# Weight sums of a seven-product matrix multiplication: which engine makes them, and the order in which they are asked for and used

## The chip, the cores and the metric

The kernel runs on one core of a Trainium2 chip. The metric is the device time of one execution in microseconds (us); it is the median over three runs. One further execution was recorded by the hardware profiler, and all rows of the profile come from that one.

## The reference

One layer of a streaming encoder for 512 frames of width 2048, in fp32. Cut to what matters:

```
h = rms_norm(x);  proj = h @ w_in
y_a = banded softmax attention (16 heads of 64, own chunk of 64 frames + 8 before)
y_g = rms_norm(gated linear attention (4 heads)) * silu(r_g)
x = x + concat(y_a, y_g) @ w_out
u = causal_depthwise_conv(rms_norm(x) @ w_ffn_up);  x = x + (gelu(u_gate) * u_val) @ w_ffn_down
x = x + sigmoid(rms_norm(x) @ w_ple_gate) * (p @ w_ple_proj)
out = rms_norm(x)
```

The matrix products are the bulk. The change concerns how the weights of some of them are prepared.

## The kernel before, in words

**A unit.** A large product is cut into units. Each unit multiplies a 2 x 2 block of weights (L11, L12, L21, L22, each 128 x 1024 values, in the down stages dn1 and dn2 128 x 896) by the stage's activations, and does so with seven products in place of eight (PRODUCTS, ahead of line 32). The products use four weight sums and seven operands that are formed once per stage:

```
P1: L11 R11   P2: L12 R21   P6: S2 N2   P5: S1 N1   P7: S3 T3   P3: S4 R22   P4: L22 T4
S1 = L21 + L22    S2 = S1 + L11    S3 = L21 + L11    S4 = S2 + L12
```

The order of the products is PLAIN (line 32): P1, P2, P6, P5, P7, P3, P4. Every weight or sum is split into a high part (`wh`, made by ScalarE, called ACT in the profile) and a low part (`wl`, the difference, made by VectorE, called DVE). A product is three passes of 8 matmuls (7 in dn1 and dn2) on TensorE (PE) into one of the accumulators accA, accB and accC.

**How a sum is made.** A unit has one of three modes, `sums`:
- "dma": SyncE (SP) loads L21 into a page, and GpSimd (POOL) issues a DMA that accumulates L22 (for S1) or L11 (for S3) onto it; so L21 comes in twice. S2 and S4 are added by VectorE.
- "dve": each L is loaded once, and VectorE adds all four sums (`make`, from line 415).
- "s3": as "dve", but S3 is made by a DMA of POOL that accumulates L11's page onto L21's page.

**Pages and the order of the loads.** Raw weights and sums live in pages of a small ring. NEEDS (line 356) gives, for each mode, the order in which a unit asks for its pages; the lists of all units are put one after another in `wanted`. `issue` (line 389) takes the next entry when a page is free and issues its load on SP and, for S1 and S3 in mode "dma", the accumulation on POOL right behind it (lines 404 to 407). A name with a star is a page that is reserved for VectorE's result. `used` (line 409) gives a page back when the last of its uses has been issued. So the order of the loads hangs on NEEDS, and the time at which each may start hangs on when VectorE or ACT has finished with an older page.

**The order of the work.** The list `steps` holds the (unit, product) pairs in order. The engines' programs are written by hand in that order: two steps ahead of a product its weights are split (`prep_high`, from line 446, then `prep_low`), one step ahead of that the next sum is added (`make`), and after a product its accumulator is collected by ACT or VectorE. An `agenda` places everything else at a step: the softmax, the stores, the loads and splits of the next stage's operands. The first two and the last two units of most stages are done in pairs, with the products of both alternating.

**The stages.** `pp` (a small projection, two units), then the front "in" with 12 units (0 to 7 give the attention's values, keys and queries, and each is followed by the softmax of its heads; 8 to 11 give the gates), `pp` again, then `wo` (output projection), `up` (44 units), `dn0`, `dn1`, `dn2` (down projection in three chunks of 8 units), and `pg` (the last gate). Before them stands the gated linear attention, in plain matmuls. The next stage's operands are loaded in the buffers that the present stage's operands leave; a load of operand T3 for `wo` waits until P7 of the front's last unit has read the old T3. A split of such an operand occupies ACT and VectorE at the step that the agenda gives it (lines 856 to 868 for the stages from `wo` on).

**Modes before.** All 12 front units are "dma". In the stages dn0 to dn2 the first two and the last two units are "dma" and the rest are "dve" (lines 832 to 834).

Of the kernel before, what the change touches and what calls it, by code (L numbers as in the profile page):

```python
# [29 lines left out]
            "P7": ("S3", "T3", "A"), "P3": ("S4", "R22", "C"), "P4": ("L22", "T4", "A"),  # L30
            "PP": ("L11", None, None)}
PLAIN = ("P1", "P2", "P6", "P5", "P7", "P3", "P4")
HALVES = ("P1", "P2", "P6", "P7", "P4", "P5", "P3")
RINGS = {"wr": ("r0", "r1", "r2"), "wh": ("h0", "h1", "h2"), "wl": ("l0", "l1", "l2")}
FRONT_RINGS = {"u": ("u0", "u1"), "c": ("c0",), "x": ("r6",)}
# [6 lines left out]
def encoder_block(ctx: ExitStack, tc: tile.TileContext, A, out):  # L42
# [13 lines left out]
    class InOrder:  # L56
        def __init__(self, engine):
            self.engine, self.on = engine, False
# [44 lines left out]
    late = []  # L103
# [103 lines left out]
    def xslot(i, name):  # L207
        return pairs[i % 8][:, i // 8, :]
# [7 lines left out]
    first = xslot(0, "x0_0")  # L216
# [50 lines left out]
    def scratch(name, shape):  # L267
        return dp.tile(list(shape), F32, name=name)
# [44 lines left out]

    class Stage:
        def __init__(self, name, units, kb, xd, weights, after, sums, edge, last=PLAIN, begin=None, begin_at=0,
                     chained=False, pace=None, late=(), single=False):
            self.name, self.kb, self.xd, self.weights, self.after = name, kb, xd, weights, after
            self.begin, self.begin_at, self.pace, self.late = begin, begin_at, pace, late
            self.chained, self.tail, self.quarter = chained, [None, None], None
            self.n = (4, kb - 4 - 2 * chained)  # L320
            self.x = {}
            n = len(units)
            self.units = [Unit(self, u, last if i >= n - 2 else PLAIN, edge if i < 2 or i >= n - 2 else sums)
                          for i, u in enumerate(units)]
            for i in range(n):
                self.units[i].pos = i
            if single:
                self.groups = [[u] for u in self.units]
                return
            self.units[0].first = True  # L330
            for i in range(2):
                self.units[i].head = i
                self.units[n - 2 + i].last = i
            self.groups = [self.units[:2]] + [[u] for u in self.units[2:-2]] + [self.units[-2:]]
# [7 lines left out]
        def split(self, op, g, body=True, tails=(0, 1)):  # L342
# [6 lines left out]
            if self.chained and g == 1:  # L349
# [4 lines left out]


    NEEDS = {"dma": ("L11", "L12", "S1", "S2*", "S3", "L22"), "dve": ("L11", "L12", "L21", "L22", "S1*", "S2*"),
             "s3": ("L11", "L12", "L21", "L22", "S1*", "S2*")}

    class Unit:
        def __init__(self, stage, u, order, sums):  # L360
            self.stage, self.u, self.order, self.sums = stage, u, order, sums
            self.first, self.head, self.last = False, None, None
            self.w, self.tag = {}, {}
            if sums == "dma":
                self.uses = dict(L11=2, L12=2, S1=2, S2=2, S3=1, L22=1)
                self.made = {"S2", "S4"}
            else:
                self.uses = dict(L11=3, L12=2, S1=2, S2=2, L21=2, L22=2)
                self.made = {"S1", "S2", "S3", "S4"}
            self.parts = dict(C11=2, C12=2, C22=2, C21=1)  # L370
            self.have = set()
            self.left = dict(A=4, B=1, C=2)
            self.o = None
            self.banks = {}
# [40 lines left out]
    def make(unit, name):  # L415
        if name not in unit.made:
            return
        unit.made.discard(name)
        n = unit.stage.kb * P
        w = lambda q: unit.w[q][:, :n]  # L420
        if name == "S1":
            vec.tensor_tensor(made_page(unit, "S1")[:, :n], w("L21"), w("L22"), ALU.add)
            used(unit, "L21")
            used(unit, "L22")
            if unit.sums == "s3":
                unit.made.discard("S3")
                nc.gpsimd.dma_start(w("L21"), w("L11"), accum_op=ALU.add)
                used(unit, "L11")
        elif name == "S2":
            make(unit, "S1")  # L430
            vec.tensor_tensor(made_page(unit, "S2")[:, :n], w("S1"), w("L11"), ALU.add)
            used(unit, "S1")
            used(unit, "L11")
        elif name == "S3":
            make(unit, "S1")
            if "S3" in unit.made or unit.sums == "dve":
                vec.tensor_tensor(w("L21"), w("L21"), w("L11"), ALU.add)
                used(unit, "L11")
        else:
            vec.tensor_tensor(w("S2"), w("S2"), w("L12"), ALU.add)  # L440
            used(unit, "L12")
# [4 lines left out]
    def prep_high(i, own=None):  # L446
        if i >= len(steps):
            return None
        unit, prod = steps[i]
        name = PRODUCTS[prod][0]  # L450
        n = unit.stage.kb * P
        make(unit, name)
        if prod == unit.order[0] and unit.sums != "dma":
            make(unit, "S1")
        if i + 1 < len(steps):
            nxt, p = steps[i + 1]
            q = PRODUCTS[p][0]
            if (nxt is unit or nxt.paired) and (q != "S4" or "P6" in nxt.w):
                make(nxt, q)
        if i > 0 and steps[i - 1][1] == "P6" and steps[i - 1][0].paired:  # L460
            make(steps[i - 1][0], "S4")
        key = {"S4": "S2"}.get(name, "L21" if name == "S3" and unit.sums != "dma" else name)
        raw = unit.w[key]
        hi, lo = own or (page("wh", "wh", F32R), page("wl", "wl", F32R))
        act.activation(hi[:, :n], raw[:, :n], AF.Copy)
        unit.w[prod] = hi, lo
        return unit, key, hi[:, :n], lo[:, :n], raw[:, :n]
# [66 lines left out]
    def load_x(src, unit):  # L534
        unit.xs = page("c", "xs").rearrange("p (s t) -> p s t", s=2)
        nc.sync.dma_start(unit.xs, src[unit.u])
# [106 lines left out]
    def after_gate(unit):  # L643
# [9 lines left out]
                    begin=lambda u: load_x(streams[0], u), begin_at=6, chained=True)]  # L653
# [13 lines left out]
    h1d = operand_scratch("h1", 8)  # L667
# [152 lines left out]
    def front_weights(u, q):  # L820
        j = {"1": u, "2": 8 + u}[q[1]] if u < 8 else 24 + 2 * (u - 8) + (q[1] == "2")
        return A["w_blk"][j, int(q[2]) - 1]

    front = Stage("in", list(range(12)), 8, h1d, front_weights, lambda u: (attend if u.u < 8 else after_gates)(u), "dma",
                  "dma", single=True)
    embed = [Stage("pp", us, 8, None, lambda u, q: A["w_ple_proj"][u], lambda u: [], "dma", "dma", single=True)
             for us in ([0, 1], [2, 3])]
    for u in embed[0].units + embed[1].units:
# [1 line left out]
    mids = streams[1:3] + [scratch("x2d_", (8, P, 2, T)), streams[3]]  # L830
    for ci, n in enumerate(CHUNKS):
        stages.append(Stage(f"dn{ci}", list(range(8)), n // 2, gd[ci], blk2(A[f"w_dn{ci}"]),
                            after_add(mids[ci + 1]) if ci < 2 else after_norm(streams[3], h3d, nple),
                            "dve", "dma", begin=lambda u, s=mids[ci]: load_x(s, u), begin_at=0 if ci else 8, late={}))
    stages.append(Stage("pg", list(range(8)), 8, h3d, blk2(A["w_ple_gate"]), after_gate, "dma", "dma", last=HALVES,
                        begin=load_gate, begin_at=9, chained=True, pace=(15, 5.3), late={}))
    stages[4].quarter = last_quarter(lambda: stages[8], nple)
# [7 lines left out]
    for st in stages:  # L845
        for group in st.groups:
            base[group[0]] = base[group[-1]] = len(steps)
            steps += [(u, p) for p in group[0].order for u in group]
            for u in group:
                u.paired = len(group) > 1  # L850
            need = [[(u, name) for name in (NEEDS[u.sums] if u.stage not in embed else ("L11",))] for u in group]
            wanted += [e for es in zip(*need) for e in es]
# [3 lines left out]
    for a, b in zip(stages[3:], stages[4:]):  # L856
        i0 = base[a.units[-1]]
        for n, p in enumerate(PLAIN):
            op = PRODUCTS[p][1]
            for g in range(2):  # L860
                start = 2 * n + 2 + g
                if g and b.chained:
                    start = max(start, 5)
                at = 2 * n + (11 if g else 8)
                if g and b.chained and op in ("R21", "T4"):
                    at = max(at, 15)
                agenda[i0 + start].append((0, lambda b=b, op=op, g=g: b.load(op, g)))
                agenda[i0 + at].append((3, lambda b=b, op=op, g=g: b.split(op, g)))

    i0 = base[front.units[-1]]  # L870
    for n, op in enumerate(("T3", "R22", "T4")):
        for g in range(2):
            agenda[n + g * (n == 2)].append((3, lambda op=op, g=g: front.split(op, g)))
    for n, p in enumerate(PLAIN):
        op = PRODUCTS[p][1]
# [4 lines left out]
        at, k = ((8, 1), (8, 1), (9, 1), (12, 1), (11, 3), (12, 3), (13, 3))[n]  # L880
# [80 lines left out]
    end = len(steps) - 14  # L961
# [6 lines left out]
    for n in range(2):  # L968
        u = stages[-1].units[n - 2]
# [292 lines left out]
    for i, (unit, prod) in enumerate(steps[:-4]):  # L1262
# [19 lines left out]
        if i - len(steps) in EARLY:  # L1282
            p, op, g = EARLY[i - len(steps)]
# [8 lines left out]
        elif prod == unit.order[-1]:  # L1292
            begin = i + 1
            if st.pace:
                begin = max(begin, base[st.units[0]] + int(st.pace[0] + st.pace[1] * unit.pos))
# [167 lines left out]
```

## Time and profile before

| | us |
|---|---|
| median of three runs | 2304.75 (2300.37 to 2307.55) |
| the profiled execution | 2304.32 |
| its span, first to last instruction | 2302.6 |
| TensorE busy | 2261.4 (98%) |
| VectorE busy | 1888.0 (82%) |
| ScalarE busy | 1300.7 (56%) |
| mean granted TensorE clock | 0.993 |

A group row of the profile reads: line, engine, operation, what is written from what with its shape, count, then total busy us and mean ns of one, then the idle time of the engine just before these instructions and what ended most of it. Line 64 is the line of the helper that records the instructions in order, so that nearly all compute instructions carry it; they are told apart by the tiles that they write and read (`s` is a page with S1 or S3 made by DMA or S2 or S4 made by VectorE; `l` a page with a loaded L; `u` a unit's result; `sc` the softmax's scores; `ptr` transposes of them on TensorE). In the rows of waits stand who waited, for what, the total, how often, and the longest. In the chain of waits stand the start in us, the duration, and what the chain passed through. In the rows of the busy times in a stretch, the numbers behind the stretch's bounds are its length, then each engine's busy time with the count of instructions, then the granted clock, the busy share of the DMA engines and GB/s.

### The profile page before, as it was taken

To read this page: it belongs to the slowest core of one execution; us is meant where nothing else is said; L and a number is where in the kernel's file an instruction comes from. 1 tells how busy PE (TensorE), PEld (TensorE's weight loads), DVE (VectorE), ACT (ScalarE), POOL (GpSimd) and SP (SyncE) were. 2 spreads that over 40 slices of the span, in tenths; PEclk is the share of its full clock that TensorE was granted. 3 is DMA by queue.
4 is the path that set the end of the run, shared out by engine and by line. 5 is a ranking of instruction groups with operands and counts; after the bars stand their busy time and mean duration, and the time that the engine had idled before them with its cause. 6 is when DMAs were issued, how large, how long until landed. Compare 5 with 4: busy or idle time off the path is not lost.

```text
span 2302.6 us, 44996 instructions
## 1 busy us (share of the span) xinstructions
PE 2261.4 (98%) x18016; PEld 2189.7 (95%) x18016; DVE 1888.0 (82%) x2590; ACT 1300.7 (56%) x1908; POOL 144.0 (6%) x181
## 2 busy tenths in 40 slices
PE   9999999999999999999999999999999999999996
PEld 8888889999989999999999999999999999999996
DVE  7566458998788888998888888888898787998986
ACT  6354456776565665555555555555564554656655
POOL 0000000000000100000000000000000100000000
PEclk9999999999999999999999999999999999999999
DMA  6623586667978977787878787777866967879994
GB/s 217 204 74 110 183 271 166 186 182 200 309 251 257 327 214 211 207 221 205 227 197 219 204 222 211 215 208 217 272 207 231 309 216 255 268 254 329 268 292 163
DMA packets 195569, 516.77 MB, mean 224 GB/s; under 512 B 20928, under 2 KB 72384, under 8 KB 195360
## 3 DMA queue, kind: packets, MB, share of 16 engines
q1 hardware_dynamic: 166080, 422.37, 52.5%
q0 software_dynamic: 23616, 84.95, 21.2%
q10 hardware_dynamic: 5664, 6.59, 0.8%
q8 instruction: 141, 2.31, 0.4%
q14 instruction: 68, 0.56, 0.1%
HBM read 435.18 MB, written 76.55 MB: 222 GB/s over the span
## 4 chain that ended last, share of the span: by engine, by line
PE 87%; DVE 6%; DMA 3%; ACT 3%; issue 2%; DVEq 0%; ACTq 0%; POOLq 0%; SPq 0%
PE accA L64 40%; PE accC L64 21%; PE accB L64 10%; PE v L252 3%; PE v L254 3%; PE v L253 3%; DVE wl L64 1%; DMA s<-in_w_blk 1%; PE py L64 1%; PE ptr L64 1%; PE psc L64 1%; DVE s L64 1%; DMA s<-in_w_out 1%; DVE u L64 1%; DVE xs L64 1%
## 5 line engine op out<-in xcount | busy, mean ns | idle before, releaser
L64 DVE TENSOR_TENSOR wl<-s,wh 128x1024 fp32r<-128x1024 f32 (+1 forms) x365 | 437.9, 1200 | 65.8 <-ACT wh L64 65.0
L64 ACT ACTIVATE wh<-l 128x1024 fp32r<-128x1024 f32 (+1 forms) x308 | 319.1, 1037 | 184.7 <-PE accC L64 118.0
L64 DVE TENSOR_TENSOR wl<-l,wh 128x1024 fp32r<-128x1024 f32 (+1 forms) x308 | 367.8, 1194 | 61.0 <-ACT wh L64 60.6
L64 ACT ACTIVATE wh<-s 128x1024 fp32r<-128x1024 f32 (+1 forms) x365 | 377.7, 1036 | 34.2 <-DVE s L64 15.8
L64 ACT ACTIVATE u<-accA 128x256 f32<-128x256 f32 x290 | 109.6, 378 | 365.4 <-PE accA L64 365.4
L64 DVE TENSOR_TENSOR s<-s,l 128x1024 f32<-128x1024 f32 (+1 forms) x192 | 229.7, 1196 | 8.5 <-DMA s<-in_w_blk 8.5
L64 PE MATMUL accA<-up_T,wh 128*128 128x256 f32 x1408 | 178.8, 279 | 0.0
L64 PEld LDWEIGHTS accA<-up_T,wh 128*128 128x128 f32 x1408 | 170.3, 188 | 0.0
L64 DVE SCALAR_TENSOR_TENSOR cv<-u,cw,cv 128x511 f32<-128x511 f32 (+1 forms) x176 | 131.7, 749 | 3.1
L407 POOL DMA_DIRECT2D s<-in_w_up x88 | 75.3, 856 | 787.9 <-DMA s<-in_w_up 383.6
L252 PE MATMUL v<-wv_h,h 128*128 128x512 f32 x256 | 100.2, 391 | 0.1
L254 PE MATMUL v<-wv_h,h 128*128 128x512 f32 x256 | 100.2, 391 | 0.0
L253 PE MATMUL v<-wv_l,h 128*128 128x512 f32 x256 | 99.7, 389 | 0.0
L64 PE MATMUL accA<-up_T,wl 128*128 128x256 f32 x704 | 96.6, 279 | 0.0
L64 PE MATMUL accA<-dn_T,wh 128*128 128x256 f32 x704 | 91.5, 282 | 4.1 <-ACT wh L64 4.1
L64 PE MATMUL accB<-up_R,wh 128*128 128x256 f32 x704 | 91.6, 282 | 2.0 <-DVE up_R L64 1.3
L64 PEld LDWEIGHTS accA<-dn_T,wh 128*128 128x128 f32 x704 | 86.8, 191 | 4.7 <-ACT wh L64 4.7
L64 PE MATMUL accA<-up_R,wh 128*128 128x256 f32 x704 | 89.8, 280 | 0.0
L64 PE MATMUL accC<-up_R,wh 128*128 128x256 f32 x704 | 89.4, 279 | 0.0
L64 PE MATMUL accA<-up_N,wh 128*128 128x256 f32 x704 | 89.4, 279 | 0.0
L64 PE MATMUL accC<-up_N,wh 128*128 128x256 f32 x704 | 89.4, 279 | 0.0
L64 PEld LDWEIGHTS accB<-up_R,wh 128*128 128x128 f32 x704 | 86.7, 190 | 2.7 <-DVE up_R L64 1.6
(401 smaller groups left out, 5070.6 us busy)
## 6 DMA issues: line engine op xcount, KB each, us to landing
l<-in_w_up SPq DMA_DIRECT2D x132, 512.0 KB, 5.5
s<-in_w_up SPq DMA_DIRECT2D x88, 512.0 KB, 4.9
s<-in_w_up POOLq DMA_DIRECT2D x88, 512.0 KB, 6.2
l<-in_w_dn SPq DMA_DIRECT2D x56, 448.0 KB, 5.7
l<-in_w_blk SPq DMA_DIRECT2D x36, 512.0 KB, 4.7
l<-in_w_out SPq DMA_DIRECT2D x28, 512.0 KB, 5.1
l<-in_w_dn SPq DMA_DIRECT2D x28, 512.0 KB, 5.3
s<-in_w_blk SPq DMA_DIRECT2D x24, 512.0 KB, 4.6
```

The source lines that it names most:

```text
L64: ins = f(*args, **kw)
L252: nc.tensor.matmul(ps[t], h1[kt][:, 0, sl], wh, start=kt == 0, stop=False)
L253: nc.tensor.matmul(ps[t], h1[kt][:, 0, sl], wl, start=False, stop=False)
L254: nc.tensor.matmul(ps[t], h1[kt][:, 1, sl], wh, start=False, stop=kt == KD - 1)
L407: nc.gpsimd.dma_start(t, src("L22" if name == "S1" else "L11"), accum_op=ALU.add)
```

## The change

It has three parts.
1. Front units 0 to 7 get the mode "first": all as in "dma", but the page for S1 is asked for ahead of L11 and L12.
2. Front units 8, 9 and 10 become "dve", unit 11 becomes "s3". Seven accumulating DMAs and four loads of 512 KB go, and VectorE makes seven more additions.
3. In all front units, and in the first two units of dn0, dn1 and dn2, P3 and P7 change places (order LATE_S3: P1, P2, P6, P5, P3, P7, P4). In the down stages the splits of R22 and T3 change places with them; the loads of these operands keep their order.

The number of matmuls, and of instructions on ScalarE, stays as it is.

```diff
 PLAIN = ("P1", "P2", "P6", "P5", "P7", "P3", "P4")
+LATE_S3 = ("P1", "P2", "P6", "P5", "P3", "P7", "P4")
...
         def __init__(self, name, units, kb, xd, weights, after, sums, edge, last=PLAIN, begin=None, begin_at=0,
-                     chained=False, pace=None, late=(), single=False):
+                     chained=False, pace=None, late=(), single=False, head=PLAIN, end=()):
...
-            self.units = [Unit(self, u, last if i >= n - 2 else PLAIN, edge if i < 2 or i >= n - 2 else sums)
+            how = [edge] * 2 + [sums] * (n - 4) + [edge] * 2
+            how[n - len(end):] = end
+            self.head = head
+            self.units = [Unit(self, u, head if i < 2 or single else last if i >= n - 2 else PLAIN, how[i])
                           for i, u in enumerate(units)]
...
     NEEDS = {"dma": ("L11", "L12", "S1", "S2*", "S3", "L22"), "dve": ("L11", "L12", "L21", "L22", "S1*", "S2*"),
+             "first": ("S1", "L11", "L12", "S2*", "S3", "L22"),
              "s3": ("L11", "L12", "L21", "L22", "S1*", "S2*")}
...
-            if sums == "dma":
+            if sums in ("dma", "first"):
                 self.uses = dict(L11=2, L12=2, S1=2, S2=2, S3=1, L22=1)
...
-        if prod == unit.order[0] and unit.sums != "dma":
+        if prod == unit.order[0] and unit.sums in ("dve", "s3"):
             make(unit, "S1")
...
-        key = {"S4": "S2"}.get(name, "L21" if name == "S3" and unit.sums != "dma" else name)
+        key = {"S4": "S2"}.get(name, "L21" if name == "S3" and unit.sums in ("dve", "s3") else name)
...
-    front = Stage("in", list(range(12)), 8, h1d, front_weights, lambda u: (attend if u.u < 8 else after_gates)(u), "dma",
-                  "dma", single=True)
+    front = Stage("in", list(range(12)), 8, h1d, front_weights, lambda u: (attend if u.u < 8 else after_gates)(u), "first",
+                  "first", single=True, head=LATE_S3, end=("dve", "dve", "dve", "s3"))
...
-                            "dve", "dma", begin=lambda u, s=mids[ci]: load_x(s, u), begin_at=0 if ci else 8, late={}))
+                            "dve", "dma", begin=lambda u, s=mids[ci]: load_x(s, u), begin_at=0 if ci else 8, late={}, head=LATE_S3))
...
-                at = 2 * n + (11 if g else 8)
+                at = 2 * b.head.index(p) + (11 if g else 8)
```

## The prediction

> **What bounds the kernel now.** I read the page first, then the waits of TensorE and VectorE, then the chain of waits around the longest of them, and last the busy time in short stretches.
>
> ```profile
> span 2302.6 us, 44996 instructions
> ...
> PE 2261.4 (98%) x18016; PEld 2189.7 (95%) x18016; DVE 1888.0 (82%) x2590; ACT 1300.7 (56%) x1908; POOL 144.0 (6%) x181
> ...
> PE 87%; DVE 6%; DMA 3%; ACT 3%; issue 2%; DVEq 0%; ACTq 0%; POOLq 0%; SPq 0%
> ```
>
> TensorE bounds the kernel: it is idle for 2302.6 - 2261.4 = 41.2 us, and nothing in the change alters a matmul. So the change can only take away or add idle time of TensorE, or time at a lower clock. The profiled run took 2304.3 us, 1.7 us beyond its span and 0.4 us below the median of 2304.75 us; I carry each change in microseconds over to the median. 0.3% (6.9 us, about what a measurement of this kernel can tell from no change) is a sixth of all idle time there is.
>
> ```profile
> PE accA L64 <- ACT wh L64: 4.1, 3, 3.0
> ...
> PE ptr L64 <- DVE sc L64: 2.0, 1, 2.0
> PE ptr L64 <- DVE mx L64: 2.0, 3, 1.6
> ...
> DVE s L64 <- DMA s<-in_w_blk: 8.5, 3, 4.1
> ```
>
> Two of these belong to sums that an accumulating DMA makes: the longest wait on ACT's wh (3.0 us), and VectorE's waits on in_w_blk (8.5 us), which reach TensorE as the 2.0 us on sc. The chain of waits shows both; first the front, in its second and third unit:
>
> ```profile
> 335.52 6.73 DMA s<-in_w_blk
> 342.34 1.24 DVE s L64
> ...
> 354.69 7.25 DMA s<-in_w_blk
> ...
> 366.11 0.50 DVE sc L64
> 366.65 1.25 PE ptr L64 x8
> ```
>
> VectorE's add S2=S1+L11 stands behind the landing of S1 at 342.3 and again at 361.9. What is queued behind it on VectorE, the softmax's sc included, comes late, and the transposes ptr start late. The second place is the head of dn2, product P7 of its second unit:
>
> ```profile
> 1984.44 7.84 DMA s<-in_w_dn
> 1992.35 0.96 ACT wh L64
> 1993.36 3.99 PE accA L64 x21
> ```
>
> S3 lands at 1992.3, ACT splits it 1 us later, and TensorE starts at 1993.36. The busy times in the stretches around both (core's columns: length, PE, PEld, DVE, ACT, POOL, granted clock, DMA share, GB/s):
>
> ```profile
> 364.60:368.00 3.40, 1.39 (x11) 1.12 (x11) 3.26 (x12) 2.43 (x7) 0.00 (x0) 1.00 0.36 139
> 368.00:371.41 3.41, 3.41 (x18) 3.41 (x18) 3.27 (x13) 3.41 (x9) 0.00 (x0) 0.50 0.02 5
> 371.41:374.80 3.39, 3.39 (x37) 3.09 (x37) 3.29 (x12) 2.73 (x10) 0.00 (x0) 1.00 0.55 142
> ...
> 1989.40:1992.80 3.40, 0.99 (x9) 0.79 (x7) 0.01 (x1) 0.45 (x1) 0.00 (x0) 1.00 0.98 316
> 1992.80:1996.20 3.40, 2.84 (x13) 2.85 (x14) 2.87 (x3) 3.40 (x6) 0.00 (x0) 0.50 0.33 84
> ```
>
> Each stall is followed by 3.4 us at half clock: 18 matmuls where the next 3.39 us hold 37. So a stall costs itself and up to half of 3.41 us: at the front 2.0 + 1.7 = 3.7 us, in dn2 3.0 + 2.84 / 2 = 4.4 us.
>
> **Part 1: S1 asked for first (front units 0 to 7).** SP's load of L21 for S1 moves past the loads of L11 and L12, and POOL's accumulation behind it starts that much sooner. The order in which a unit's pages are asked for puts S1 three product steps ahead of before, 8.4 us or more by this row for one product (the next rows are the landings):
>
> ```profile
> 319.65 2.80 PE accA L64 x24
> ...
> s<-in_w_blk SPq DMA_DIRECT2D x24, 512.0 KB, 4.6
> ...
> l<-in_w_blk SPq DMA_DIRECT2D x36, 512.0 KB, 4.7
> ```
>
> VectorE's longest wait was 4.1 us, so all go, and TensorE's 2.0 us with the half clock: -3.7 us. Bounds: -2.0 if the clock drops all the same, -3.7. What comes late next is L11, now behind 512 KB more; a unit's seven products alone take 7 x 2.80 = 19.6 us, against 4.7 us to landing, so I leave it at nothing. If it did land late, ACT's split of it and then P1, the first product, would be held once in each unit, with all that ACT and VectorE have queued behind.
>
> **Part 2: P3 ahead of P7 in the front.** S4 = S2+L12 is wanted one product sooner, and its add (1.2 us by the row below) moves on VectorE ahead of the softmax's normalisation; ACT's split of S4 moves with it, S3's back. No instruction is added. The stretch rows tell how much room VectorE has:
>
> ```profile
> 370.00:550.00 180.00, 180.00 (x1619) 174.72 (x1618) 162.00 (x404) 130.79 (x268) 11.96 (x14) 1.00 0.69 184
> ...
> 550.00:644.00 94.00, 90.87 (x718) 86.53 (x717) 69.92 (x119) 58.53 (x92) 6.19 (x8) 0.98 0.90 282
> ...
> L64 DVE TENSOR_TENSOR s<-s,l x192: 1082/1218/1226, 319.6 to 2249.5; 128x1024 f32<-128x1024 f32 x160, 128x896 f32<-128x896 f32 x32
> ...
> L64 DVE TENSOR_TENSOR s<-l,l x16: 1083/1152/1221, 678.1 to 2054.8; 128x1024 f32<-128x1024 f32 x8, 128x896 f32<-128x896 f32 x8
> ```
>
> In steady attention TensorE never idles while VectorE is 90% busy (162 of 180 us). What stands behind the moved add comes 1.2 us later unless VectorE had a gap; the bounds are 0 and 7 units x 1.2 = 8.4 us. The 18 us of gaps are twice the work moved, so I take a value near 0: a twelfth, +0.7.
>
> **Part 3: gate units 8 to 11 sum on VectorE.** Seven accumulations leave POOL and four loads leave SP, 11 transfers of 512 KB; VectorE gains seven adds of 1.15 to 1.22 us, 8.3 us in all (unit 11's S3 stays a DMA of POOL, now from one page to another). From 550 to 644 it has 24 us free, but not evenly:
>
> ```profile
> 540.13 1.22 DVE L64 TENSOR_TENSOR wl<-s,wh 128x1024 fp32r<-128x1024 f32 x1
> ...
> 541.24 0.81 PE L64 MATMUL ptr<-ident,sc 128*128 128x128 f32 x6
> ...
> 562.12 1.23 DVE L64 TENSOR_TENSOR u<-u,on 128x1024 f32<-128x1024 f32 x1 [2.01 <-ACT u L64]
> ...
> 569.40:572.80 3.40, 1.59 (x11) 1.15 (x11) 3.26 (x10) 2.83 (x7) 0.00 (x0) 1.00 1.03 364
> 572.80:576.20 3.40, 3.40 (x18) 3.40 (x17) 1.61 (x2) 0.25 (x1) 0.85 (x1) 0.50 1.04 333
> ```
>
> Units 8 and 9 are prepared while the last softmaxes still run: ptr at 541 follows VectorE's normalisation within 1 us, and around 571 TensorE already waits for VectorE (1.8 us idle, then half clock). Four of the adds (S1 and S3 of both units) fall there, 4.8 us; the one gap of 2.0 us takes some. Bounds: 0 (all in gaps) and 4.8 plus one more half-clock stretch, 6.5. I take 2.2, nearer the low end because 24 us are free in the whole stretch; the three adds of units 10 and 11 fall after the softmaxes and cost nothing. L22 is now needed for the first sum, and VectorE waits with it if it lands late; that is inside the bounds.
>
> [...]
>
> **Part 4: the start of wo.** wo's load of T3 waits until the front's last unit has used that buffer in P7, now one product (2.8 us) later, and SP's loads of R22 for wo queue behind it. Against it stand the 11 transfers less before.
>
> ```profile
> 644.00:660.00 16.00, 12.13 (x95) 11.13 (x94) 16.00 (x24) 12.32 (x22) 0.64 (x1) 1.00 0.81 253
> ...
> PE accA L64 <- DVE wl L64: 2.4, 2, 1.3
> ```
>
> TensorE is idle for 3.9 us here with VectorE busy in all 16.0 us, so VectorE is the limit and the transfers come second. Bounds: -3.9 and +2.8; I take 0.
>
> **Part 5: P3 ahead of P7 in the first two units of each down stage.** In dn2 P7 of the second unit moves back by one pair of products, 2 x 21 matmuls, or 2 x 21/24 x 2.80 = 4.9 us. P7 would come at about 1993.4 - 3.0 + 4.9 = 1995.3; S3 landed 3.0 us before that, and ACT's split of it took 0.96 us. The stall and its half clock go: -4.4 us (0 if S4 or R22 is late instead). R22's split takes T3's slot on ACT and T3's goes later; SP's loads keep their order. In dn1's head TensorE never idles, though VectorE is busy for 23.6 of 24 us (first row): 0. The other rows are for dn0:
>
> ```profile
> 1836.00:1860.00 24.00, 24.00 (x208) 24.00 (x207) 23.61 (x28) 16.82 (x23) 0.00 (x0) 1.00 0.94 302
> ...
> 1692.00:1701.00 9.00, 6.92 (x53) 6.11 (x52) 8.36 (x10) 7.41 (x10) 0.00 (x0) 1.00 0.38 137
> ...
> 1676.72 1.04 ACT L64 ACTIVATE dn_T<-dn_T 128x1024 fp32r<-128x1024 f32 x1
> ...
> L340 SPq DMA_DIRECT2D dn_R<-g_R x2: 319/428/538, 1663.8 to 1664.3; - x2
> ...
> dn_R<-g_R SPq DMA_DIRECT2D x2, 512.0 KB, 13.2
> ```
>
> R22's split moves into the slot at 1676.72 that T3 had, while R22 lands about 13.2 us after 1663.8, at 1677: no margin, and ACT would hold the next unit's wh for a few tenths. TensorE's 2.1 us of idle time lie under VectorE's 93%, and the exchange takes no work from VectorE. Bounds -2.1 and +1.5; I take 0.
>
> **Sum.** -3.7 + 0.7 + 2.2 + 0 - 4.4 + 0 = -5.2 us: 2299.1 us against the profiled run, 2299.5 against the median. Its own range is -8.1 + 2.9 with parts 2 to 4 varied by 3 either way: 2296.5 to 2302.5.
>
> **Rivals.** (a) VectorE has room everywhere: parts 2 and 3 cost nothing, and the emptier queues give back half of wo's 3.9 us. Then -8.1 - 1.9 = -10.0 us, 2294.7 (2292.7 with all of it). For it: 24 us free from 550 to 644; against: the 571 stall. (b) Slower: VectorE takes the bound from TensorE in the front. If S4's add shows in full in seven attention units (7 x 1.2 = 8.4) and the four adds of units 8 and 9 too (4.8), that is 13.2 - 8.1 = +5.1 us, 2309.9, with one half-clock stretch more 2311.6. It decides once 8.1 of these 13.2 us show on TensorE; the 10% VectorE has free speak against it, the late softmax at 366 and 571 for it. (c) In the down stages the wait only changes its name: P3 waits for R22 or S4 as P7 did for S3. Then part 5 gives nothing: -0.8 us, 2304.0. R22's margin in dn0 speaks for it; dn2, where VectorE was idle (0.01 of 3.40 us), against. (d) The clock drops do not come from the stalls, so only 2.0 + 3.0 go: -5.0 + 2.9 = -2.1, 2302.7. Against it stand both pairs of rows. [...]
>
> **How the numbers follow.** Forecast 0.40, (a) 0.34, (b) 0.14, (c) 0.08, (d) 0.04. Below 2297.8 (-0.3%) lie (a) and 0.08 of the forecast's own range: faster 0.42. Above 2311.7 lie the worse part of (b), with L11 or R22 late on top, and little else: slower 0.12. The rest, 0.46, is within 0.3%. The range runs from (a) with all of wo's idle time, just above 2292.5, to 2308.0 between the forecast and (b).
>
> **What would show it.** Right: VectorE's wait on in_w_blk under 1 us, no clock drop at 368 or at dn2's head, TensorE waiting 1 to 3 us more for sc, mx or PT between 540 and 575, seven adds of 1.15 to 1.22 us more. Wrong: waits on l<-in_w_blk before a unit's P1; TensorE idle in steady attention by more than 2 us; waits for dn_R or s in the heads of dn0 to dn2; wo's start idle by under 2 or over 6 us.

## The result: slightly slower, outside the range

The changed kernel is slower: the ratio to the kernel before is 1.0024, with a 95% interval of 1.0012 to 1.0035, that is +5.5 us (2.8 to 8.1). The medians over 22 runs each are 2313.35 us (2305.42 to 2318.23) and 2310.86 us (2299.14 to 2315.35). The forecast was 2299.5 us with a range of 2292.5 to 2308.0.

The median of before stood at 2304.75 us over its first three runs; repeated runs of one kernel spread over some 16 us, and 7 us of that can come from a stage that the change leaves alone (last section). So besides the ratios I compare profiles stage by stage, a stage being taken from the start of its first matmul to that of the next stage's. For example, from two views by tile (engine, operation, count: duration in ns, first and last start in us), first before, then after:

```profile
L64 PE MATMUL accA<-in_R,wh x192: 277/279/282, 319.5 to 608.1; 128*128 128x256 f32 x192
...
L64 PE MATMUL accA<-wo_R,wh x128: 277/280/282, 638.6 to 766.1; 128*128 128x256 f32 x128
```

```profile
L65 PE MATMUL accA<-in_R,wh x192: 277/280/283, 319.2 to 614.1; 128*128 128x256 f32 x192
...
L65 PE MATMUL accA<-wo_R,wh x128: 277/280/281, 646.5 to 773.0; 128*128 128x256 f32 x128
```

The front (with the small projection behind it) took 638.6 - 319.5 = 319.1 us before and 646.5 - 319.2 = 327.3 us after. From the page, one row of before, then after:

```profile
L64 DVE TENSOR_TENSOR s<-s,l 128x1024 f32<-128x1024 f32 (+1 forms) x192 | 229.7, 1196 | 8.5 <-DMA s<-in_w_blk 8.5
```

```profile
span 2313.8 us, 44976 instructions
...
PE 2269.6 (98%) x18016; PEld 2197.8 (95%) x18016; DVE 1899.3 (82%) x2597; ACT 1301.5 (56%) x1908; POOL 138.0 (6%) x174
...
L65 DVE TENSOR_TENSOR s<-s,l 128x1024 f32<-128x1024 f32 (+1 forms) x192 | 229.6, 1196 | 0.9 <-DMA s<-in_w_dn 0.7
```

The change does what it says: seven more instructions on VectorE, seven fewer on POOL, and VectorE's idle time in front of its adds on the accumulating DMA fell from 8.5 to 0.9 us. TensorE's waits tell where the loss is (the first row is before, the others after):

```profile
PE accC L64 <- ACT u L64: 0.5, 1, 0.5
```

```profile
PE accC L65 <- ACT u L65: 6.3, 6, 3.8
...
PE accA L65 <- DVE u L65: 4.0, 4, 1.9
...
PE ptr L65 <- DVE mx L65: 3.1, 3, 1.6
```

The waits on sc and on ACT's wh (2.0 and 4.1 us before) are gone, as forecast, and the softmax waits 3.1 us for VectorE's mx (2.0 before). In the place of the former stand two groups that before were 0.5 us (on accC) and absent (on accA): accC behind ACT's u, and accA behind VectorE's u. `u` is the unit's result, so these are matmuls that wait until the product before them has been taken out of the accumulator. The table of products says why. Each accumulator is summed up over several products: P3 is added onto P5's result in accC, and P4 onto P7's in accA, and in between the partial sum has to be read out. In PLAIN the last products take accC, accA, accC, accA by turns; in LATE_S3 they are accC, accC, accA, accA. The engine that reads out then works while TensorE stands still.

How long depends on what that engine has queued. TensorE, VectorE at P4 of a gate unit (timelines, of the same execution):

```profile
583.57 1.09 PE L65 MATMUL accA<-in_T,wl 128*128 128x256 f32 x8
586.53 3.42 PE L65 MATMUL accA<-in_T,wh 128*128 128x256 f32 x16 [1.87 <-DVE u L65]
```

```profile
582.24 1.22 DVE L65 TENSOR_TENSOR s<-l,l 128x1024 f32<-128x1024 f32 x1
583.37 0.75 DVE L65 TENSOR_TENSOR tp<-yp 128x256 f32<-128x256 f32 x2
584.04 0.88 DVE L65 SCALAR_TENSOR_TENSOR tp<-tp,yp 128x256 f32<-128x256 f32 x2
584.84 1.22 DVE L65 TENSOR_TENSOR wl<-l,wh 128x1024 fp32r<-128x1024 f32 x1
585.97 0.41 DVE L65 TENSOR_TENSOR u<-u,accA 128x256 f32<-128x256 f32 x1
```

P7 ends at 584.66. VectorE is on a run of older work, one of the new additions (s<-l,l) in it, and reaches the 0.41 us read of accA at 585.97. The longest such wait is at the head of dn0, where ACT takes P5 out of accC:

```profile
1708.52 0.63 ACT L65 ACTIVATE cv<-cv 128x512 f32<-128x512 f32 x1 [1.58 <-DVE cv L65]
1709.05 1.04 ACT L65 ACTIVATE dn_T<-dn_T 128x1024 fp32r<-128x1024 f32 x1
1710.00 0.36 ACT L65 ACTIVATE u<-accC 128x256 f32<-128x256 f32 x1
```

```profile
1705.53 1.10 PE L65 MATMUL accC<-dn_N,wl 128*128 128x256 f32 x8
1710.41 3.45 PE L65 MATMUL accC<-dn_R,wh 128*128 128x256 f32 x16 [3.78 <-ACT u L65]
```

Even with two units in alternation, ACT reaches the read only after the last conv work of the stage up and an operand's split. And two of these stalls cost clock besides (columns as in the prediction); the wait of 2.4 us at the last gate unit's P4, at 632, cost none (granted clock 1.00 from 628 to 634.8):

```profile
583.60:587.04 3.44, 1.57 (x14) 1.39 (x13) 3.41 (x7) 1.06 (x1) 0.00 (x0) 0.98 0.99 320
587.04:590.45 3.41, 3.41 (x18) 3.41 (x18) 1.61 (x2) 0.00 (x0) 0.00 (x0) 0.52 0.75 238
1706.50:1709.91 3.41, 0.13 (x2) 0.00 (x0) 3.02 (x4) 1.83 (x3) 0.00 (x0) 1.00 0.25 97
1709.91:1713.32 3.41, 2.90 (x13) 2.91 (x14) 3.16 (x4) 3.41 (x6) 0.00 (x0) 0.50 0.41 154
```

### The profile page after: what moved, and what is told of

Read it like the earlier page. It is cut to its first block, busy times and chain, and to the rows that moved or that the text cites. A ratio compares the mean times of both kernels' runs of the same rounds, so it can differ in the third digit from the quotient of the medians.

```text
span 2313.8 us, 44976 instructions
## 1 busy us (share of the span) xinstructions
PE 2269.6 (98%) x18016; PEld 2197.8 (95%) x18016; DVE 1899.3 (82%) x2597; ACT 1301.5 (56%) x1908; POOL 138.0 (6%) x174
## 4 chain that ended last, share of the span: by engine, by line
PE 85%; DVE 6%; ACT 4%; DMA 3%; issue 1%; ACTq 0%; SPq 0%; DVEq 0%
PE accA L65 40%; PE accC L65 21%; PE accB L65 10%; PE v L253 3%; PE v L255 2%; PE v L254 2%; DVE wl L65 2%; PE py L65 1%; ACT wh L65 1%; DVE s L65 1%; DVE u L65 1%; PE psc L65 1%; PE ptr L65 1%; DMA xs<-x1d 1%; DMA x3d<-xs 0%
## 5 line engine op out<-in xcount | busy, mean ns | idle before, releaser
L65 DVE TENSOR_TENSOR wl<-s,wh 128x1024 fp32r<-128x1024 f32 (+1 forms) x361 | 432.6, 1199 | 67.9 <-ACT wh L65 67.0
L65 DVE TENSOR_TENSOR wl<-l,wh 128x1024 fp32r<-128x1024 f32 (+1 forms) x312 | 372.5, 1194 | 63.0 <-ACT wh L65 62.8
L65 DVE TENSOR_TENSOR u<-u,accC 128x256 f32<-128x256 f32 x98 | 41.0, 418 | 61.9 <-PE accC L65 60.6
L65 PEld LDWEIGHTS accA<-up_T,wl 128*128 128x128 f32 x704 | 89.1, 188 | 0.0
```

The lines of the kernel that those rows point to most:

```text
L65: ins = f(*args, **kw)
```

## The experiments

Theory A is the accumulators, as above. Theory B is VectorE's extra work, rival (b) of the prediction; theory C, in one run, a load that lands late. The edits of x1, x3, x6, x7 and x8 are shown against the changed kernel, those of x2, x5 and x9 against the kernel before, with lines that only define a name left out. x0, x5 and x7 to x10 are one execution each; with a spread of 16 us their times alone tell little, and I go by the stages. The table holds all profiles, stage by stage, in us (front with the small projections; "rest" is from pg's first matmul to the end of the span).

| kernel | front | wo | up | dn0 | dn1 | dn2 | rest |
|---|---|---|---|---|---|---|---|
| before | 319.1 | 162.2 | 868.9 | 161.3 | 137.2 | 142.4 | 192.0 |
| x0, before again | 315.2 | 162.1 | 876.1 | 161.3 | 137.2 | 140.5 | 192.1 |
| after | 327.2 | 161.5 | 875.9 | 162.4 | 137.2 | 137.9 | 192.5 |
| x10, after again | 325.5 | 161.7 | 875.9 | 163.9 | 137.2 | 137.9 | 193.8 |
| x1, parts 1 and 2, old order | 315.6 | 162.3 | 876.0 | 161.3 | 137.2 | 143.0 | 192.0 |
| x2, new order, old sums | 320.9 | 160.5 | 876.0 | 163.9 | 138.5 | 139.1 | 191.8 |
| x3, x1 and new order in dn2 | 316.8 | 163.9 | 875.9 | 161.3 | 137.2 | 137.9 | 194.3 |
| x5, part 2, old order | 320.0 | 161.2 | 868.5 | 161.3 | 137.2 | 142.8 | 192.5 |
| x6, part 1 and new order in dn2 | 313.3 | 162.0 | 876.2 | 161.3 | 137.2 | 138.6 | 193.6 |
| x7, another late order in front | 324.6 | 160.1 | 876.0 | 162.6 | 137.2 | 137.9 | 192.7 |
| x8, new order in units 0 to 7 and dn2 | 318.4 | 162.6 | 876.5 | 161.3 | 137.2 | 137.9 | 192.7 |
| x9, before, new order in up | 320.0 | 163.2 | 933.5 | 161.3 | 137.2 | 138.8 | 191.8 |

The front's times hold stretches of 3.41 us at half clock (0.50 in the rows of the prediction, 0.52 at 587 above), each worth up to 1.7 us by an estimate from these rows: two in before, after, x7 and x9, one in x10, x3 and x5, none in x0, x1, x2, x6 and x8. A comparison of two fronts with unequal numbers of them mixes the clock with the waits; I say so where it matters.

**x0 and x10: both kernels once more.** No edit.

> The kernel before, unchanged, for a second profile. Every theory expects the idle places of the first profile again (front 2.0 us at the transposes near 366, head of dn2 3.0 us) and no wait at the exchanged products. It tells what of the difference between the two profiles is not the change: the stage up ran at 116.67 us per 1000 matmuls before and 117.76 after, 7.4 us over the stage. If that step belongs to single executions, it may show up here too.

2305.49 us. The front was 3.9 us shorter than in the first profile, against the expectation: TensorE did not wait near 366. VectorE still waited for the same transfers, 5.7 us in place of 7.9 up to 372:

```profile
DVE s L64 <- DMA s<-in_w_blk: 9.8, 4, 4.2
...
PE ptr L64 <- DVE mx L64: 2.0, 3, 1.6
```

```profile
364.60:368.00 3.40, 3.40 (x28) 3.04 (x27) 3.26 (x12) 2.44 (x6) 0.00 (x0) 1.00 0.03 10
```

So VectorE's waits reach TensorE in some executions (this one not, nor x2 in the new order; the first profile and x5 and x9, which hold the same sums in this place, did) and are hidden in others. Up ran at the longer of two times, as in after; so this is not the change.

> The changed kernel again, for a second profile. Theory A: the waits on the two accumulators stand at the same places with the same lengths within 0.2 us (339: 0.77, 587: 2.0, 609: 0.77, 632: 2.5, dn0: 3.9 us); front 325 to 328 us. Theory B (they come from transfers that land late in one execution): other places or lengths.

2316.77 us. The waits stood where they had stood: in starts of matmuls, 0.77 us late at 338.6, 2.03 at 584.8, 0.77 at 607.7, 2.53 at 630.6, 3.94 at 1708.8 (after: 0.77, 2.03, 0.77, 2.53, 3.95). They come from the order, not from one execution's transfers.

**x1: the order put back everywhere.**

```diff
-                  "first", single=True, head=LATE_S3, end=("dve", "dve", "dve", "s3"))
+                  "first", single=True, end=("dve", "dve", "dve", "s3"))
...
-                            "dve", "dma", begin=lambda u, s=mids[ci]: load_x(s, u), begin_at=0 if ci else 8, late={}, head=LATE_S3))
+                            "dve", "dma", begin=lambda u, s=mids[ci]: load_x(s, u), begin_at=0 if ci else 8, late={}))
```

> The changed kernel with the order of products put back everywhere (parts 1 and 2 alone). Theory A (accumulators): in the new order P3 follows P5 in accC and P4 follows P7 in accA, so TensorE waits until the first result is taken out; with the order back all these waits go (front and gate units -8.7 us of idle time, dn0 -3.9 us and its old 2.7 us back), while the S3 wait of dn2 comes back (+3.0 and half clock): about 8 us faster than after, 4 us faster than before. Theory B (VectorE has too much to do in the gate units): the waits between 575 and 645 stay, since the seven additions stay; within 2 us of after. Theory C (a late load of L11): waits on l<-in_w_blk at the start of units stay.

Ratio to before 1.000 (0.9984 to 1.0016), median 2308.03 us; the gain of 4 us against before did not show. Against after, the medians differ by 5.3 us, where 8 were expected. The front fell from 327.2 to 315.6 us, -11.6, with all waits on accC and accA behind a `u` gone from the gate units though VectorE still makes the seven additions: theory B is out for these. Of theory C's kind there is one wait, of ACT for 1.0 us on a loaded L, and none of TensorE behind it. The one line left of both groups:

```profile
PE accC L65 <- ACT u L65: 0.5, 1, 0.5
```

Dn2's stall is back (143.0 us), dn0's four short ones too. Of the 11.6 us, 3.4 are the two half-clock stretches of after, one of which (573) stands behind a softmax stall that before has too; x10 against x3, with one such stretch each, gives 8.7. So in this kernel the new order cost the front 8 to 9 us and clock besides, and parts 1 and 2 together gave nothing that the timing can tell.

**x2: the new order with the old sums.**

```diff
-                  "dma", single=True)
+                  "dma", single=True, head=LATE_S3)
...
-                            "dve", "dma", begin=lambda u, s=mids[ci]: load_x(s, u), begin_at=0 if ci else 8, late={}))
+                            "dve", "dma", begin=lambda u, s=mids[ci]: load_x(s, u), begin_at=0 if ci else 8, late={}, head=LATE_S3))
```

> The kernel before with the order of products exchanged, and the modes of the sums as before (part 3 alone). Theory A: the waits at P3 and P4 in units 0, 1 and 8 to 11 and in the head of dn0 show as in after, though VectorE has none of the seven additions: 0.6 to 0.8 us each where the engine that takes the result out has nothing else, 2 to 4 us where it is behind; slower than before by 5 us or more. Theory B: no such waits in the gate units; at least the 3 us of dn2 gained, faster than before.

Ratio 1.0013 (0.9997 to 1.0029), median 2310.36 us: +3.0 us (-0.7 to 6.7), where 5 or more were expected; the timing leaves it unclear, and the stages decide. The waits are there without the additions on VectorE:

```profile
PE accC L65 <- ACT u L65: 6.0, 6, 3.8
...
PE accA L65 <- DVE u L65: 1.9, 3, 0.7
```

On accC they are as in after (6.3); on accA 1.9 us against 4.0. At the first gate unit's P4 the matmul is 0.89 us late in place of 2.03, and no clock drop follows (granted clock 1.00 from 583.6 to 593.9). VectorE's queue ahead of that read is the one shown for after without the addition s<-l,l of 1.22 us:

```profile
578.54 0.42 DVE L65 TENSOR_TENSOR u<-u,accC 128x256 f32<-128x256 f32 x1 [1.88 <-PE accC L65]
578.88 0.75 DVE L65 TENSOR_TENSOR tp<-yp 128x256 f32<-128x256 f32 x2
```

So the order alone makes the wait, and an addition in VectorE's queue lengthens it at this place: there parts 2 and 3 of the change add to more than their sum. At the last gate unit's P4 the wait is 2.53 us in both kernels.

**x3: parts 1 and 2, new order in dn2 alone.**

```diff
-                            "dve", "dma", begin=lambda u, s=mids[ci]: load_x(s, u), begin_at=0 if ci else 8, late={}, head=LATE_S3))
+                            "dve", "dma", begin=lambda u, s=mids[ci]: load_x(s, u), begin_at=0 if ci else 8, late={}, head=LATE_S3 if ci == 2 else PLAIN))
```

with the front as in x1.

> Parts 1 and 2, and the exchanged order in the head of dn2 alone (front, dn0 and dn1 in the old order). Theory A: no wait at P3 or P4 in the front or in dn0, the wait on S3 in dn2 gone; faster than before by 6 to 9 us, the forecast that I had made for the whole change. Theory B: the gate units cost 3 to 6 us, no gain against before.

Ratio 0.9991 (0.9975 to 1.0007), median 2304.70 us: -2.1 us, where 6 to 9 were expected. Dn2 took 137.9 us. In all profiles, the five with the old order there took 138.8 to 143.0 us, mean 141.5, and the seven with the new one 137.9 to 139.1, mean 138.2: a gain of 3.3 us. The lowest of the five, 138.8 us in x9, has no stall on S3, with the old order too. The front did not gain against x0.

**x7: another order with S3 as late.**

```diff
+SPREAD = ("P1", "P5", "P6", "P2", "P3", "P7", "P4")
...
-                  "first", single=True, head=LATE_S3, end=("dve", "dve", "dve", "s3"))
+                  "first", single=True, head=SPREAD, end=("dve", "dve", "dve", "s3"))
```

> The changed kernel with another order in the 12 front units, P1 P5 P6 P2 P3 P7 P4: S3 is used as late as in the change, but P6 and P2 lie between P5 and P3 in accC; P7 and P4 still follow one another in accA. Theory A (each product waits until the one before it in the same accumulator is taken out): the 0.63 us waits at P3 (near 332, 353, 603, 624) go, the 0.77 us and longer waits at P4 (near 339, 587, 609, 632) stay; front stage 2 to 4 us shorter than the 327.2 us of after, and over 319 us. Theory B (too many additions on VectorE, or sums wanted too early): S1 is wanted two products sooner, so the waits grow in the gate units and appear at P5.

2312.33 us; the front took 324.6 us, 2.6 less than after. What is left on accC are two waits, the 3.8 us of dn0 and 0.4 us in dn2, where the product before is in accA and which the kernel before has too; those on accA stayed:

```profile
PE accA L66 <- DVE u L66: 7.3, 5, 3.2
...
PE accC L66 <- ACT u L66: 4.2, 2, 3.8
```

The 7.3 us on accA hold the last gate unit's P4, which in after the profile put down to ACT's wo_N; in starts of matmuls the waits at P4 grew from 7.3 to 8.2 us. So in the front TensorE waits for the read of an accumulator only where two of its products follow one another.

**x8: the new order where the softmax runs.**

```diff
-            self.units = [Unit(self, u, head if i < 2 or single else last if i >= n - 2 else PLAIN, how[i])
+            self.units = [Unit(self, u, (PLAIN if single and i >= 8 else head) if i < 2 or single else last if i >= n - 2 else PLAIN, how[i])
```

with the down stages as in x3.

> Parts 1 and 2, the exchanged order in front units 0 to 7 and in the head of dn2; units 8 to 11, dn0 and dn1 in the old order. Theory A: in units 2 to 7 the softmax's matmuls lie between the products, so that the exchange costs nothing there; waits only in units 0 and 1 (0.63 + 0.77 + 0.63 us) and none from 575 on: front 317 to 319 us. Theory B (VectorE late in attention through S4's earlier addition): over 321 us with waits at ptr and py.

2307.60 us, front 318.4 us. In starts of matmuls: 0.63, 0.77 and 0.64 us in units 0 and 1, then 0.1 and 1.1 us in two of the six units with a softmax, no wait on a neighbour from 575 on. Where the softmax's matmuls lie between the neighbours, most of the read is hidden; I had expected all of it.

**x9: the cost by itself, in a stage that the change leaves alone.**

```diff
-            self.units = [Unit(self, u, last if i >= n - 2 else PLAIN, edge if i < 2 or i >= n - 2 else sums)
+            self.units = [Unit(self, u, last if i >= n - 2 else LATE_S3 if name == "up" and i >= 2 else PLAIN, edge if i < 2 or i >= n - 2 else sums)
```

> The kernel before with the exchanged order in the 40 middle units of the stage up, where the change had left it alone; sums as before. Theory A: each unit pays for two neighbours in one accumulator, at least 0.63 + 0.77 = 1.4 us, and more where ACT or VectorE is behind: 56 to 120 us more than the 869 to 876 us of this stage. Theory B: the order costs nothing where no addition is added, below 5 us.

2367.06 us; up took 933.5 us, 57.5 more than the 876 of most profiles (64.6 more than 868.9). The waits, 40 of each in up (the 41st on accC is in dn2):

```profile
PE accA L65 <- DVE u L65: 24.8, 40, 0.7
PE accC L65 <- ACT u L65: 19.4, 41, 0.5
```

```profile
860.00:960.00 100.00, 94.51 (x790) 92.84 (x791) 81.12 (x95) 51.51 (x69) 8.54 (x10) 1.00 0.69 189
```

A pair of neighbours costs 0.47 us as a wait on ACT and 0.62 us on VectorE; between the starts of the matmuls the gaps are longer, 0.63 and 0.77 us, since a matmul's row lasts 0.28 us and the next one starts after 0.12 us where nothing waits (859 in 100 us, last section): 1.40 x 40 = 56 us of the 57.5, the low end of what was expected. VectorE is less busy than in the same stretch before (81.12 against 88.45 us), so it did not become the bound.

**x6: part 1 and dn2's head alone.** As x3, with the sums of units 8 to 11 by DMA:

```diff
-                  "first", single=True, head=LATE_S3, end=("dve", "dve", "dve", "s3"))
+                  "first", single=True, end=("dma", "dma", "dma", "dma"))
```

> Part 1 (S1 asked for first) and the exchanged order in the head of dn2 alone, all sums as before. The four gate units keep their accumulating DMAs. Theory A: no wait at exchanged products, front 315 to 317 us, dn2 2.5 to 4.5 us shorter than before: 2304 us, 3 to 6 us below the kernel before. If part 2 gives something, this is slower than the run with parts 1 and 2 and dn2.

Ratio 0.9967 (0.9951 to 0.9984), median 2303.31 us: -7.6 us (-11.3 to -3.7) against before, the best of all, and faster than the change as a whole. The front, 313.3 us, is the shortest seen: 1.9 us under x0, 5.8 under the first profile. Against x1 and x3 (315.6, 316.8) it tells the price of part 2, 2.3 to 3.5 us; x3 has one half-clock stretch and the others none, so that 1.8 to 2.3 us are waits.

**x5: part 2 alone.**

```diff
-                  "dma", single=True)
+                  "dma", single=True, end=("dve", "dve", "dve", "s3"))
```

> Part 2 alone: the kernel before, with the sums of the four gate units on VectorE, products in the old order. The front stage took 315.2, 319.1 and 320.0 us in three profiles with the sums of before (the longer two with the wait on VectorE's sc near 366), 313.3 us with part 1 and 315.6 and 316.8 us with parts 1 and 2. Theory A: part 2 costs 2 to 3.5 us at the last softmaxes (530 to 575) and nothing after 575: front 317 to 323 us, as the stall near 366 comes or not. Theory B (the additions also cost in the gate units): over 323 us, with waits between 575 and 645.

2305.28 us, front 320.0 us with the stall near 366. That is 0.9 us more than before and as much as x9, which have the same sums but two half-clock stretches where x5 has one; with these taken out at 1.7 us each, part 2 costs 2.6 and 1.7 us, much as in the comparison with x6. The last softmaxes wait 3.4 us on VectorE's mx in place of 2.0; from 575 to 645 no wait comes that before does not have.

```profile
PE ptr L65 <- DVE mx L65: 3.4, 4, 1.6
PE ptr L65 <- DVE sc L65: 2.3, 1, 2.3
```

## Why the prediction was wrong, point by point

**The step that failed** is the one on P3 ahead of P7 in the front ("No instruction is added"; +0.7 us, bounds 0 to 8.4). I weighed the move by VectorE's work and never looked into which accumulator each product writes, although the products' table names it. What it adds is a wait, not an instruction. The runs showed 5.7 us in the front with the old sums (x2 against x0, neither with a half-clock stretch nor the stall near 366) and 8.7 to 11.6 us with the new ones (x10 against x3, after against x1), clock included. In starts of matmuls nine waits in the front of after add to 9.9 us, and one of 1.4 us at the small projection behind them goes. Rival (b) gave a loss of about the right size, but by a mechanism that x1 contradicts: the additions stayed and the loss went. None of my rivals was this one. The 40 units of x9 show the same wait in a stage that the change leaves alone, at 1.4 us a unit.

**Dn0 in part 5** (0, bounds -2.1 to +1.5): I looked at R22's landing. Dn0 took 162.4, 163.9, 163.9 and 162.6 us with the new order (after, x10, x2, x7), 161.3 without: +1.1 to +2.6 us. Five short stalls of 3.6 to 3.9 us together went, and one of 3.9 us at P3, behind ACT's conv work, came, with half clock behind it; the loss is of the size of that clock, 1.7 us a stretch.

**Dn2 in part 5** (-4.4 us): right in mechanism, and three quarters of it in size, 3.3 us in the mean; the stall differs from one execution to the next.

**Part 1** (-3.7 us): VectorE's waits in these units went, as forecast: POOL's accumulation for the second unit was issued at 327.0 us in place of 335.5. But what they cost TensorE near 366 is 2.2 to 2.7 us in the first profile, x5 and x9, with a clock drop in two of the three, and nothing in x0. x6's front against x0 and the first profile gives -1.9 to -5.8 us; of the -1.9, 1.1 us is a wait of x0 at 588, in a gate unit that part 1 leaves alone.

**Part 2, called part 3 in the forecast** (+2.2 us): 1.7 to 2.6 us without the clock (x1 and x3 against x6, x5 against before and x9), at the softmaxes as forecast, and with no waits in the gate units by itself.

**The start of wo** (0): 0.4 to 0.7 us shorter, the two profiles of after against the two of before. But the last front unit's P4 waits 2.4 us just ahead of it, since VectorE has wo's operands to split before it reads accA; the profile puts that wait down to ACT's wo_N, but the read of accA ends 0.1 us before the matmul starts.

**The clock** (rival (d), 0.04): the half-clock stretches went with the old stalls and came with the new ones, at 587 and 1710 (granted clock 0.52 and 0.50). Rival (d) is out. But the forecast's step that each stall is followed by half clock was too simple: the stall near 366 in x5 is longer than in the first profile (2.5 against 2.2 us) and cost none, the granted clock staying at 1.00:

```profile
365.41:368.82 3.41, 1.72 (x12) 1.38 (x12) 3.27 (x11) 2.43 (x5) 0.00 (x0) 1.00 0.33 131
368.82:372.24 3.42, 3.42 (x29) 3.34 (x28) 3.28 (x13) 3.42 (x10) 0.00 (x0) 1.00 0.02 5
```

The wait of 2.4 us at 632 in after cost no clock either. So a stall holds a clock share, by the estimate up to 1.7 us, only where the rows of its execution show one; what tells such a stall from one that costs no clock is left open here.

**The sum**, from the table, after against the second profile of before (both have up at 876): front +12.0, wo -0.6, dn0 +1.1, dn2 -2.5, up and the rest +0.2, together, with the 0.1 us by which the front starts sooner, the 10.0 us between the spans 2303.8 and 2313.8. x10 against the first profile, without up: +6.4 - 0.5 + 2.6 - 4.5 + 1.8 = +5.8. The timing's +5.5 (2.8 to 8.1) lies at the lower of the two. Most of the difference is in the front: the stall near 366, which x0 does not have, and the half-clock stretches. How often each of them comes was not measured.

## What to carry to other kernels

When products are reordered, write down for each neighbour pair which accumulator it uses: two in a row that share one put the whole read-out, and everything queued ahead of it on the reading engine, on TensorE's path, here mostly 0.63 to 0.77 us each and up to 3.9 us behind a busy reader. A change made of several parts is worth taking apart: the exchange in the head of dn2 and S1 asked for first gained, and the exchange elsewhere ate both. A wait that one profile shows on the critical path may be hidden in the next execution, as the 2.2 us near 366 in the first profile and none in x0; two profiles of the kernel before would have told that part 1 was worth less than it looked.

## What was not expected of the hardware

The stage up ran at one of two paces. Of eleven profiles besides x9, two took 868.9 and 868.5 us and nine took 875.9 to 876.5. TensorE waits for nothing in the stretches below and its granted clock is 1.00, yet 100 us hold 859 matmuls in one and 852 in the other (before, then x0):

```profile
860.00:960.00 100.00, 100.00 (x859) 100.00 (x858) 88.45 (x106) 55.71 (x75) 8.56 (x10) 1.00 0.76 208
```

```profile
860.00:960.00 100.00, 100.00 (x852) 100.00 (x851) 89.27 (x108) 54.99 (x74) 9.39 (x11) 1.00 0.76 207
```

That is 0.8%, 7 us over the stage, more than the whole effect of the change, and it appears with the same kernel (before and x0) and on the same chip (x5 with 868.5 us, x10 with 875.9). Its cause is open. Anyone who compares single executions of such a kernel would take it for an effect of the edit.
